# Both merge gates of a hybrid layer by a seven-product scheme, with block sums made in DRAM

## The chip, the core and the metric

The kernel runs on one core of a Trainium2 chip. The metric is the device time of one execution in microseconds (us); of several runs the median counts. One execution was also recorded by the hardware profiler, and the views of the profile quoted below are of that one.

## The reference

One layer over 512 tokens of width 1024, in float32. A gated linear recurrence (HGRN2, eight heads) and a latent attention (MLA, eight heads) run side by side on the same normed input, and two sigmoid gates of the input merge them:

```python
h   = rms_norm(x)                       # (512, 1024)
P   = h @ W_in                          # q | f | i | z_a | c_q | c_kv | k_rope | z_b | gate logits (2 * 1024)
y_a = HGRN2(q, f, i)  * silu(z_a)
y_b = MLA(c_q, c_kv, k_rope) * silu(z_b)
m   = sigmoid(g_a) * (y_a @ W_pa) + sigmoid(g_b) * (y_b @ W_pb)
out = rms_norm(x + m @ W_out)
```

## The kernel before

Every float32 operand of a large product is held as two parts, hi (rounded) and lo (the rest), and each product is three matmuls: hi by hi, hi by lo, lo by hi (`mm3`, L88). Activations are split once; `hT` is the normed input, channels on partitions, as such a pair. Weights come in pieces of 512 KB through `load_w` (L96): SP issues the transfer into one of three raw buffers (L110), ACT casts the hi part into one of four (L113), DVE subtracts to get the lo part into one of four (L114). The lines of these three steps appear in the profile for nearly every weight of the kernel.

The work goes in stages: the norm and the small compressed projection; four pairs of recurrence heads (`hg_pair`, L562: forget, value, query and gate projections, then decays, states, scores and outputs); eight attention heads (the loop at L744); the first merge gate (`gates`, L709), whose first quarter lies inside the last attention head; the product of y_a with w_pa; four steps that each do a quarter of the second gate and a quarter of y_b with w_pb (`merge`, L938); the product with w_out; the last norm.

A quarter of a gate is one `proj_ch` (L122): 256 output channels, two weight pieces, 48 matmuls that are 512 tokens wide. A gate is four of these, 192 matmuls.

The products with w_pa (`ch_product`, L870) and with w_out (`product`, L993) are already done by a seven-product scheme (Strassen's, in Winograd's form): the weight matrix and the activations are cut into 2 x 2 blocks, four sums of weight blocks and four sums of token blocks are formed, and seven products of blocks take the place of eight. For w_pa each block product is 48 matmuls of 256 tokens, seven of them 336 matmuls. The sums of weight blocks are made in SBUF: SP loads blocks into four buffers (`load_block`, L785), and POOL issues transfers that add one buffer onto another (`add_by_dma`, L800); `w_parts` (L804) then splits a sum.

What sets the order: a scheduler orders each engine's instructions by a model of time, within the limits of buffers and dependences. Places marked `manual_schedule` keep the written order, for TensorE nearly everywhere late in the kernel. `tc.issue_after(x)` keeps a transfer from being placed ahead of x. SP's queue carries the weight loads in the order in which they are issued; POOL computes small steps of its own (the scaled keys and queries of the recurrence at L472 and L484, the rope at L617 to L619, the scaling of the attention's probabilities at L683) and issues the adding transfers between them.

Of the kernel before, what the change touches and what calls it, by code (L numbers as in the profile page):

```python
# [38 lines left out]
def hybrid_layer(ctx: ExitStack, tc: tile.TileContext, a):  # L39
# [56 lines left out]
    def load_w(*pieces, lo_eng=None):  # L96

        raw = wraw.tile([P, WCH], F32, tag="raw", name="w_raw")
        hi = whi.tile([P, WCH], F32R, tag="hi", name="w_hi")
        lo = wlo.tile([P, WCH], F32R, tag="lo", name="w_lo")  # L100
# [13 lines left out]
        (lo_eng or nc.vector).tensor_tensor(lo[:, :o], raw[:, :o], hi[:, :o].bitcast(F32), op=ALU.subtract)  # L114
# [36 lines left out]
    last_split = [None]  # L151

    def split(hi, lo, src):

# [1 line left out]
        nc.vector.tensor_tensor(lo, src, hi.bitcast(F32), op=ALU.subtract)  # L156
# [319 lines left out]
    def hg_query(h, pq, pr):  # L476
# [7 lines left out]
        nc.gpsimd.tensor_tensor(c2_(q64), c4(qi)[:, :, 2:4], bc(gh, 10, 2), op=ALU.mult)  # L484
# [77 lines left out]
    def hg_pair(pair, before_gate=None, last=None):  # L562
        cc, hs = pair * 256, (2 * pair, 2 * pair + 1)
        pf = proj_ch(w_in, COL_F + cc, hT)
        kk = [hg_forget(h, pf[i]) for i, h in enumerate(hs)]
        def gate():
# [98 lines left out]
    def mla_scores(h, pool, qn, kn, qp, final=False):  # L665

        pn = []
        for i in range(NT):
# [40 lines left out]
    def gates(b, c, hook=None, to=None):  # L709

        res = []
        for i, ps in enumerate(proj_ch(w_in, COL_G + b * D + c * 256, hT, hook)):
            j = 8 * b + 2 * c + i
            g = z_tile()[:] if to is None else to[:, 2 * c + i]
            nc.scalar.activation(g, ps[:], AF.Tanh, scale=0.5, bias=hb_gate[:, j : j + 1])
            res.append(g)
        return res
# [434 lines left out]
```

## Time and profile before

| | |
|---|---|
| median of three runs | 619.11 us (618.95 to 619.19) |
| the profiled execution's own time | 619.32 us |
| its span, first to last instruction | 617.6 us |
| mean granted TensorE clock | 0.997 |
| TensorE (PE) busy | 607.3 us, 98% |
| weight loads (PEld) busy | 518.2 us, 84% |
| VectorE (DVE), ScalarE (ACT), GpSimd (POOL) busy | 400.5, 260.4, 117.9 us |
| transfers | 72.35 MB, mean 117 GB/s |

How to read the views. A group of instructions is one row: line, engine, operation, output <- inputs, shapes, count | busy time, mean ns of one | idle time of the engine just before, and what ended it. The waits of an engine are rows "engine, its output, line <- what it waited for: us in total, times, longest". The chain in order of time gives start, length and the instructions of each piece. A table by stage has for each stretch: its length, busy time of each engine with its instruction count in brackets, the TensorE clock, the share of the 16 DMA engines and GB/s. DMA queues are given with packets, MB and share of the 16 engines' time; DMA issues with KB each and the median us from issue to landing.

### The profile page before, as it was taken

The page shows a single profiled execution, that of the slowest core. Times are in us where ns is not written, and L with a number is a line of the kernel's source. Part 1 is how long each engine was busy: PE and PEld are TensorE (multiplying, and loading weights), DVE is VectorE, ACT ScalarE, POOL GpSimd, SP SyncE. Part 2 cuts the span into 40 slices and gives each one's busy share as a digit, 9 for nine tenths or more (in the row PEclk, how much of TensorE's full clock was granted, in tenths as well). Part 3 has the DMA queues.
Part 4 walks back from the last instruction along what each step waited for, and adds up shares of the span by engine and source line. Part 5 has one row for each costly group of instructions (what it writes and reads, how often), then busy time and mean ns, then how long its engine had stood idle before and what let it go on. Part 6 is the DMA issues. An engine that isn't in the chain of part 4 may idle for free.

```text
span 617.6 us, 8947 instructions
## 1 busy us (share of the span) xinstructions
PE 607.3 (98%) x3400; PEld 518.2 (84%) x3400; DVE 400.5 (65%) x633; ACT 260.4 (42%) x483; POOL 117.9 (19%) x219
## 2 busy tenths in 40 slices
PE   8999999999999999999999999999999999999995
PEld 4998888888888888888888888888899888888884
DVE  7727855498874639967677757458267742447895
ACT  5645143323144232346545555354354532334352
POOL 3106201231230032321314132101110012000021
PEclk9999999999999999999999999999999999999998
DMA  8325243223205202432232243239952799600403
GB/s 275 117 67 171 68 140 100 68 69 103 69 12 160 80 24 59 116 86 74 72 99 74 55 117 88 70 84 325 239 148 51 270 359 276 193 1 0 171 0 136
DMA packets 62377, 72.35 MB, mean 117 GB/s; under 512 B 6104, under 2 KB 48510, under 8 KB 62336
## 3 DMA queue, kind: packets, MB, share of 16 engines
q1 hardware_dynamic: 58476, 61.37, 31.9%
q0 software_dynamic: 2160, 7.87, 6.4%
q10 hardware_dynamic: 1700, 2.56, 1.4%
q8 instruction: 26, 0.43, 0.3%
q14 instruction: 15, 0.12, 0.1%
HBM read 60.25 MB, written 2.10 MB: 101 GB/s over the span
## 4 chain that ended last, share of the span: by engine, by line
PE 96%; DVE 2%; ACT 1%; DMA 0%; issue 0%; POOL 0%; POOLq 0%; ACTq 0%; DVEq 0%
PE mm_ps L90 23%; PE mm_ps L91 23%; PE mm_ps L92 23%; PE ax_ps L878 6%; PE ax_ps L986 4%; PE ax_ps L675 2%; PE mm_ps L266 2%; PE ax_ps L696 1%; PE ax_ps L536 1%; PE ax_ps L92 1%; PE ax_ps L91 1%; PE ax_ps L90 1%; PE mm_ps L878 1%; PE mm_ps L986 1%; PE ax_ps L538 1%; PE ax_ps L498 1%
## 5 line engine op out<-in xcount | busy, mean ns | idle before, releaser
L114 DVE TENSOR_TENSOR w_lo<-w_raw,w_hi 128x1024 fp32r<-128x1024 f32 (+3 forms) x86 | 101.8, 1187 | 104.9 <-ACT w_hi L113 97.7
L113 ACT CAST w_hi<-w_raw 128x1024 fp32r<-128x1024 f32 (+3 forms) x86 | 85.0, 991 | 160.0 <-PE mm_ps L91 89.7
L90 PE MATMUL mm_ps<-hT,w_hi 128*128 128x512 f32 x384 | 151.2, 394 | 0.0
L91 PE MATMUL mm_ps<-hT,w_hi 128*128 128x512 f32 x384 | 150.0, 391 | 0.0
L92 PE MATMUL mm_ps<-hT,w_lo 128*128 128x512 f32 x384 | 149.6, 391 | 0.0
L92 PEld LDWEIGHTS mm_ps<-hT,w_lo 128*128 128x128 f32 x384 | 72.1, 188 | 14.8
L90 PEld LDWEIGHTS mm_ps<-hT,w_hi 128*128 128x128 f32 x384 | 72.2, 188 | 14.5 <-DVE qn L156 0.2
L91 PEld LDWEIGHTS mm_ps<-hT,w_hi 128*128 128x128 f32 x384 | 72.2, 188 | 14.2
L92 PE MATMUL mm_ps<-w_hi,hT 128*128 128x512 f32 (+1 forms) x96 | 36.6, 383 | 0.0
L91 PE MATMUL mm_ps<-w_lo,hT 128*128 128x512 f32 (+1 forms) x96 | 36.5, 382 | 0.0
L90 PE MATMUL mm_ps<-w_hi,hT 128*128 128x512 f32 (+1 forms) x96 | 36.4, 386 | 0.0
L683 POOL TENSOR_SCALAR p<-p,sm 128x128 f32<-128x128 f32 (+3 forms) x28 | 17.0, 608 | 71.1 <-DVE sm L680 60.6
L681 ACT ACTIVATE p<-ax_ps,sm 128x128 f32<-128x128 f32 (+3 forms) x32 | 16.9, 530 | 28.0 <-DVE sm L680 26.5
L455 DVE RECIPROCAL tf<-pr 128x512 f32<-128x512 f32 x8 | 26.8, 3351 | 0.2
L90 PE MATMUL mm_ps<-yb,w_hi 128*128 128x512 f32 x64 | 24.9, 389 | 0.0
L91 PE MATMUL mm_ps<-yb,w_hi 128*128 128x512 f32 x64 | 24.9, 389 | 0.0
L92 PE MATMUL mm_ps<-yb,w_lo 128*128 128x512 f32 x64 | 24.9, 389 | 0.0
L90 PE MATMUL mm_ps<-cT,w_hi 128*128 128x512 f32 x52 | 20.7, 398 | 0.0
L92 PEld LDWEIGHTS mm_ps<-w_hi,hT 128*128 128x128 f32 x96 | 18.0, 188 | 3.0
L90 PEld LDWEIGHTS mm_ps<-w_hi,hT 128*128 128x128 f32 x96 | 18.0, 188 | 3.0
L91 PEld LDWEIGHTS mm_ps<-w_lo,hT 128*128 128x128 f32 x96 | 18.0, 188 | 2.9
L92 PE MATMUL mm_ps<-cT,w_lo 128*128 128x512 f32 x52 | 20.3, 390 | 0.0
(284 smaller groups left out, 1147.1 us busy)
## 6 DMA issues: line engine op xcount, KB each, us to landing
w_raw<-w_in SPq DMA_DIRECT2D x58, 512.0 KB, 3.8
x<-w_proj_a SPq DMA_DIRECT2D x10, 512.0 KB, 6.5
x<-x POOLq DMA_DIRECT2D x8, 512.0 KB, 9.4
w_raw<-w_proj_b SPq DMA_DIRECT2D x8, 512.0 KB, 9.9
w_raw<-w_proj_a SPq DMA_DIRECT2D x4, 512.0 KB, 11.2
ya<-w_out SPq DMA_DIRECT2D x4, 512.0 KB, 7.7
t<-w_out SPq DMA_DIRECT2D x4, 512.0 KB
yb<-w_out SPq DMA_DIRECT2D x4, 512.0 KB, 10.9
```

The lines of the kernel that those rows point to most:

```text
L90: nc.tensor.matmul(ps, lh[lsl], rh[rsl], start=start, stop=False)
L91: nc.tensor.matmul(ps, lh[lsl], rl[rsl], start=False, stop=False)
L92: nc.tensor.matmul(ps, ll[lsl], rh[rsl], start=False, stop=stop)
L113: nc.scalar.copy(hi[:, :o], raw[:, :o])
L114: (lo_eng or nc.vector).tensor_tensor(lo[:, :o], raw[:, :o], hi[:, :o].bitcast(F32), op=ALU.subtract)
L266: nc.tensor.matmul(ps, hT[l][:, 4 * kh + k, t * P : t * P + P], c_hl[kh][r][:, k * 256 : k * 256 + 256], start=kh == 0 and kind == 0 and k ...
L455: nc.vector.reciprocal(rp[:], pr[:])
L675: nc.tensor.matmul(sps[:, :n], qh[:, bl], kpe[x][:, :n], start=False, stop=x == 1)
L681: nc.scalar.activation(p[:, :n], sps[:, :n], AF.Exp, scale=SCALE, bias=sm[:, 1:2], accum_out=sm[:, 2:3])
L683: (nc.vector if final else nc.gpsimd).tensor_scalar(p[:, :n], p[:, :n], sm[:, 3:4], 0.5, op0=ALU.mult, op1=ALU.mult)
L878: nc.tensor.matmul(ps[:, o], w[k // 2][i][:, k % 2, cols], ap[j][:, k], start=not banks and c == 0 and n == 0, stop=n == 11, skip_group_ch ...
L986: nc.tensor.matmul(ps[:, o : o + n], ap[i][:, k, t * P : t * P + P], w[k // 2][j][:, k % 2, o : o + n], start=fresh and c == 0, stop=c == ...
```

## The change

Both gates are computed by the seven products. One helper, `strassen`, runs the seven block products for gate 0, gate 1 and w_pa, one after the other; w_pb then runs alone in four steps that merge, and w_out follows as before.

- **Sums of weight blocks, in DRAM.** For both gates, w_pa and w_out a `BlockSums` holds four 1 MB tiles in DRAM. `start` copies a block of the weights into each, by eight transfers of 512 KB from DRAM to DRAM on SP's queue. `add` puts an adding transfer (DRAM onto DRAM, 512 KB) on POOL's queue. Copies for gate 0 start after pair 0, for gate 1 after pair 1, for w_pa after pair 2, for w_out at attention head 1. Adds are spread over pairs 1 to 3 (gates) and heads 1 to 6. The sums are then loaded and split like any weight, through `load_w`.
- **Sums of token blocks of h, in DRAM.** `early_sums` forms them in two halves of channels, after the forget gates of pair 0 and after pair 0: twelve DVE operations and four casts each half. SP stores them (16 stores of 256 KB). After the last attention head POOL loads them back (eight loads of 512 KB).
- The sums of y's token blocks are made between gate 0 and gate 1. A gate's tanh is taken per 256 tokens. The adding transfers in SBUF, their four buffers and `w_parts` are gone; x for the residual and the output rows go into the buffers of y_a and y_b.

In the built programs 512-wide matmuls go from 1983 to 1599 and 256-wide from 520 to 1192.

```diff
+    class BlockSums:
...
+        def start(self):
+            with tc.issue_after(last_dma[0].ins):
+                for t, ij in zip(self.t, TERMS):
+                    for q in kh:
+                        nc.sync.dma_start(t[:, q], self.w[ij][:, q])
+        def add(self, *ns):
+            with tc.issue_after(last_pool[0].ins):
+                for n in ns:
+                    x = {0: self.w[0, 1], 2: self.w[1, 1], 1: self.t[0], 3: self.t[1]}[n]
+                    for q in kh:
+                        nc.gpsimd.dma_start(self.t[n][:, q], x[:, q], accum_op=ALU.add)
...
+    def early_sums(q):
...
+        e22, e21, e11, e12 = whole("qr", h22), whole("qs", h21), whole("qh", h11), whole("p3", h12)
+        minus(e22, e22, e21)
+        keep(1, "qn", e22)
+        minus_minus(e22, e22, e11)
+        keep(2, "kn", e22)
+        minus(e21, e11, e21)
+        keep(3, "qp", e21)
+        minus_minus(e12, e12, e22)
+        keep(4, "qn", e12)
+    steps = {("f", 0): lambda: early_sums(kh[0]),
+             ("f", 1): lambda: gate_w[0].add(0, 2), ("q", 1): lambda: gate_w[0].add(1), ("f", 2): lambda: gate_w[0].add(3),
+             ("q", 2): lambda: gate_w[1].add(0, 2), ("f", 3): lambda: gate_w[1].add(1), ("q", 3): lambda: gate_w[1].add(3),
+             ("h", 1): lambda: pa_w.add(0, 2), ("h", 2): lambda: pa_w.add(1), ("h", 3): lambda: pa_w.add(3),
+             ("h", 4): lambda: out_w.add(0, 2), ("h", 5): lambda: out_w.add(1), ("h", 6): lambda: out_w.add(3)}
...
+    def strassen(w, ops, out, pool, first=None, between={}):
...
+        r = ch_product(w.sum(1), s1, copied("c22", -1.0, pool))
+        ch_product(w.sum(2), s2, copied("c12", -1.0, pool), u)
+        ch_product(w.block(1, 1), s4, closed("c12", 4, 0, -1.0, out), r)
+        ch_product(w.sum(3), s3, closed("c22", 4, 1, -1.0, out), u)
+        ch_product(w.sum(4), y22, lambda b, ps: out(2 * b, 1, two(ps)), u)
...
-                first_gates = gates(0, 0, lambda: pts.extend(hook()))
+                u = ch_product(w11, h11, copied("c11", 1.0))
+                ch_product(w21, h12, lambda b, ps: later.append((b, ps)), tile=mm_tile, hook=lambda: pts.extend(hook()))
                 mla_out(h, pts, v, z)
...
+    for n, s in ((1, s1), (2, s2), (4, s4), (3, s3)):
+        for i in range(2):
+            nc.gpsimd.dma_start(s[i][:], h_dram[n - 1][i][:])
...
+        strassen(gate_w[0], h_ops, gate_out(0, lambda j: ma[:, j]), gp, first=u)
...
+        strassen(gate_w[1], h_ops, gate_out(1, lambda j: g1[j]), gp,
...
+        strassen(pa_w, (q1, q2, q3, s1, s2, s3, s4), gated, gp)
...
-        for i, (g, ps) in enumerate(merge(1, c, ybs, a["w_proj_b"][0])):
+        for i, ps in enumerate(proj_ch(a["w_proj_b"][0], c * 256, ybs)):
```

The order on three engines changes where the steps were put in. On SP, around the end of pair 0: before, the loads of the weights of pair 0's last projections and of pair 1's first ones follow one another (w_raw is a raw buffer).

```order
L110 DMA w_raw<-w_in 128x4x256 [waits DMAHW2_49,DVE_49]
L110 DMA w_raw<-w_in 128x4x256 [waits DMAHW3_49,DVE_49]
L110 DMA w_raw<-w_in 128x4x256 [waits DMAHW4_49,DVE_49]
L110 DMA w_raw<-w_in 128x4x256 [waits DMAHW5_49,DVE_49]
L110 DMA w_raw<-w_in 128x4x256 [waits DMAHW6_49,DVE_49]
```

In the changed program (g_t is a DRAM tile of gate 0's sums, h a DRAM tile of token sums, qn and kn what is stored) the same place reads:

```order
L110 DMA w_raw<-w_in 128x4x256 [waits DMAHW3_49,DVE_49]
L738 DMA g_t_647<-w_in 128x2x512 [waits DMAHW4_49]
L775 DMA h_666<-kn_808 128x512 [waits DMAHW5_49,DVE_49]
L738 DMA g_t_647<-w_in 128x2x512 [waits DMAHW6_49]
L738 DMA g_t_648<-w_in 128x2x512 [waits DMAHW7_49]
L738 DMA g_t_648<-w_in 128x2x512 [waits DMAHW0_49]
L738 DMA g_t_649<-w_in 128x2x512 [waits DMAHW1_49]
L738 DMA g_t_649<-w_in 128x2x512 [waits DMAHW2_49]
L775 DMA h_670<-qn_822 128x512 [waits DMAHW3_49,DVE_49]
L738 DMA g_t_650<-w_in 128x2x512 [waits DMAHW4_49]
L738 DMA g_t_650<-w_in 128x2x512 [waits DMAHW5_49]
L110 DMA w_raw<-w_in 128x4x256 [waits DMAHW6_49]
```

The last row is pair 1's first weight piece: all eight copies of gate 0 and two stores have moved in between it and the last load of pair 0.

On DVE, in pair 0, behind the forget gates of its second head: before, the key scalings are followed by the lo parts of the query weights and by the query steps (L481 to L485).

```order
L455 RECIPROCAL tf<-pr 128x512 [waits DVE_49]
L470 TENSOR_TENSOR ki<-k,tf 128x512 [waits DVE_49]
L471 TENSOR_TENSOR ko<-ki,pr 128x512 [waits DVE_49]
L473 TENSOR_TENSOR k_759<-ko,gh_641 128x512 [waits DVE_49,Pool_49]
L114 TENSOR_TENSOR w_lo<-w_raw,w_hi 128x1024 [waits DMAHW2_49,Activation_49]
L114 TENSOR_TENSOR w_lo<-w_raw,w_hi 128x1024 [waits DMAHW3_49,Activation_49]
```

In the changed program the sums (L720, L724, L768) and their lo parts (L156) stand between the same steps:

```order
L455 RECIPROCAL tf<-pr 128x512 [waits DVE_49]
L724 SCALAR_TENSOR_TENSOR qr<-qr,qh 128x512 [waits DVE_49]
L156 TENSOR_TENSOR qp_815<-qs,qp_814 128x512 [waits Activation_49]
L470 TENSOR_TENSOR ki<-k,tf 128x512 [waits DVE_49]
L724 SCALAR_TENSOR_TENSOR p_797<-p_797,qr 128x512 [waits DVE_49]
L768 TENSOR_TENSOR qh<-hT_125,hT_126 128x512
L114 TENSOR_TENSOR w_lo<-w_raw,w_hi 128x1024 [waits DMAHW2_49,Activation_49]
L768 TENSOR_TENSOR qs<-hT_125,hT_126 128x512 [waits DVE_49]
L156 TENSOR_TENSOR kn_808<-qr,kn_807 128x512 [waits Activation_49]
L471 TENSOR_TENSOR ko<-ki,pr 128x512 [waits DVE_49]
```

The two lo parts of the query weights now come behind eight to ten further rows. Some twenty rows on, ahead of the second head's query step (L483), stands the lo part of the second half's first sum, which waits for a store to be done (DMAHW3 is the semaphore of the store of h_670 above):

```order
L502 SCALAR_TENSOR_TENSOR st<-st,ft,ax_ps 128x128 [waits DVE_49]
L156 TENSOR_TENSOR qn_1253<-qr,qn_1252 128x512 [waits DMAHW3_49]
L483 TENSOR_TENSOR qi<-f,pr 128x512 [waits DVE_49]
```

So the query's scaling, qi, is queued behind that store.

On POOL, in pair 3 and ahead of the first head's rope: before, the scaled keys and queries and the rope follow one another.

```order
L472 TENSOR_TENSOR k_2212<-ko,gh_641 128x256 [waits DVE_49,PE_49]
L484 TENSOR_TENSOR q_2352<-qi,gh_637 128x256 [waits DVE_49]
L484 TENSOR_TENSOR q_2361<-qi,gh_641 128x256 [waits DVE_49]
L617 TENSOR_TENSOR qr<-qr,qtab 128x512 [waits DMAHW3_49,DMAHW5_49,DMAHW2_49,DMAHW7_49,DMASW0_49,Activation_49]
L618 TENSOR_TENSOR qs<-qs,qtab 128x512
```

In the changed program (line numbers of the rope are two higher) four adding transfers of gate 1 stand between them, each waiting for transfers that it reads or adds onto (DMASW are those of POOL's queue):

```order
L472 TENSOR_TENSOR k_2346<-ko,gh_643 128x256 [waits DVE_49,PE_49]
L745 DMA g_t_652<-g_t_651 128x1024 [waits DMAHW6_49,DMASW1_49]
L745 DMA g_t_652<-g_t_651 128x1024 [waits DMAHW7_49,DMASW2_49]
L484 TENSOR_TENSOR q_2488<-qi,gh_639 128x256 [waits DVE_49]
L484 TENSOR_TENSOR q_2497<-qi,gh_643 128x256 [waits DVE_49]
L745 DMA g_t_654<-g_t_652 128x1024 [waits DMAHW2_49,DMASW7_49,DMASW5_49]
L745 DMA g_t_654<-g_t_652 128x1024 [waits DMAHW3_49,DMASW6_49,DMASW0_49]
L619 TENSOR_TENSOR qr<-qr,qtab 128x512 [waits DMAHW5_49,DMAHW3_49,DMAHW7_49,DMAHW2_49,Activation_49]
```

Queries and rope now stand behind the waits of those four.

More of the change, by code (lines that the diff above doesn't have):

```diff
@@ L94, in hybrid_layer, with load_w @@
     last_dma = [None]
[L96 removed]
+    def load_w(*pieces, to=None):
         raw = wraw.tile([P, WCH], F32, tag="raw", name="w_raw")
[L99 to L100 removed]
+        hi, lo = to or [pool.tile([P, WCH], F32R, tag=tag, name=f"w_{tag}")[:] for pool, tag in ((whi, "hi"), (wlo, "lo"))]
         views, o = [], 0
@@ L706, in mla_out @@
         nc.vector.tensor_tensor(yb[:, h], ops[:], z[:], op=ALU.mult)
[L709 to L717, printed above, removed]
+    kh = [slice(0, 2), slice(2, 4)]
+    half_t = [slice(0, 256), slice(256, 512)]
@@ L719, in hybrid_layer, with step, beside @@
+    def step(*at):
+        if at in steps:
+            steps[at]()
+    def beside(pair):
+        if pair < 2:
+            gate_w[pair].start()
+        if pair == 0:
+            early_sums(kh[1])
+        if pair == 2:
+            pa_w.start()
     for pair in range(H // 2 - 1):
         hg_pair(pair)
+        beside(pair)
     early = []
@@ new lines, in hybrid_layer, with copied, done, closed @@
+    two = lambda ps: ps[:].rearrange("p (c t) -> p c t", c=2)
+    part = {}
+    def copied(key, sign, pool=None):
+        def done(b, ps):
+            if b == 0:
+                t = pool.tile([P, WCH], F32, "part", 2) if pool else wraw.tile([P, WCH], F32, tag="raw", name=key)
+                part[key] = t[:].rearrange("p (b c t) -> p b c t", b=2, c=2)
+            nc.scalar.activation(part[key][:, b], two(ps), AF.Copy, scale=sign)
+        return done
+    def closed(key, j, tok, sign, out):
+        def done(b, ps):
+            t = part[key][:, b]
+            nc.vector.scalar_tensor_tensor(t, two(ps), sign, t, op0=ALU.mult, op1=ALU.add)
+            out(j + 2 * b, tok, t)
+        return done
@@ L739, in hybrid_layer @@
+    h11, h12, h21, h22 = zip(*[blocks(t) for t in hT])
     mw = Pool("mla", "right")
@@ new lines, in hybrid_layer, with gate_out, out @@
+    q1, q2, q3 = [[yo.tile([P, 4, 256], F32R, f"q{n}{i}") for i in range(2)] for n in range(1, 4)]
+    mp = Pool("merged", "left")
+    ma = mp.tile([P, KD, S], F32, "ma")
+    gp = Pool("gates", "left")
+    g_rows = gp.tile([P, 5, S], F32, "g_rows")
+    def gate_out(b, rows):
+        def out(j, tok, src):
+            for i in range(2):
+                n = 8 * b + j + i
+                nc.scalar.activation(rows(j + i)[:, half_t[tok]], src[:, i], AF.Tanh, scale=0.5, bias=hb_gate[:, n : n + 1])
+        return out
@@ new lines, in hybrid_layer @@
+    g1 = {j: z_tile()[:] for j in (0, 1, 4)}
+    for n, j in enumerate((2, 3, 5, 6, 7)):
+        g1[j] = g_rows[:, n]
+    with tc.manual_schedule(engines={mybir.EngineType.PE}):
+        strassen(gate_w[1], h_ops, gate_out(1, lambda j: g1[j]), gp,
+                 between={3: lambda: a_parts(y22, s1), 4: lambda: a_parts(y11, s2), 5: lambda: a_parts(y12, s4),
+                          6: lambda: a_parts(y21, s3)})
+    ybs = hT
+    for h in range(H):
+        split(ybs[0][:, h], ybs[1][:, h], yb[:, h])
```

273 lines of the change are left out of this document (113 added, 160 removed).

## The prediction

> **What bounds the kernel now.** I read the summary first, then the chain of work that ended last by engine.
>
> ```profile
> span 617.6 us, 8947 instructions
> PE 607.3 (98%) x3400; PEld 518.2 (84%) x3400; DVE 400.5 (65%) x633; ACT 260.4 (42%) x483; POOL 117.9 (19%) x219
> ...
> PE 96%; DVE 2%; ACT 1%; DMA 0%; issue 0%; POOL 0%; POOLq 0%; ACTq 0%; DVEq 0%
> ```
>
> TensorE is busy for 98% of the span and carries 96% of the chain. Next, the waits of TensorE, all of them:
>
> ```profile
> PE ax_ps L231 <- DVE zero L277: 1.2, 1, 1.2
> PE ax_ps L255 <- DVE xn L247: 0.8, 2, 0.4
> PE mm_ps L266 <- DVE w_lo L238: 0.5, 1, 0.5
> PE mm_ps L266 <- ACT hT L257: 0.2, 1, 0.2
> ```
>
> Together 2.7 us, every one at lines of the opening (norm, transposes, first projection). From there to the last product TensorE never waits. So a change pays exactly the matmul time it removes, less whatever waits it brings into a stream that has none. Last, the chain in order of time, through the one matrix product that is already done by seven products at 256 tokens (L878), and the first products of the output projection (L986), whose matmuls are 512 wide:
>
> ```profile
> 444.45 5.75 PE ax_ps L878 x48
> 450.20 5.76 PE mm_ps L878 x48
> 455.96 25.92 PE ax_ps L878 x216
> ...
> 482.58 2.87 PE ax_ps L878 x24
> ...
> 571.84 5.44 PE ax_ps L986 x24
> 577.28 5.44 PE mm_ps L986 x24
> 582.72 21.77 PE ax_ps L986 x96
> ```
>
> The seven products are 48 + 48 + 216 + 24 = 336 matmuls in 5.75 + 5.76 + 25.92 + 2.87 = 40.30 us, 119.9 ns each. A 512-wide matmul takes 5.44 / 24 = 226.7 ns. Half the width costs 53% of the time, not 50%.
>
> **The gain.** A gate now is four pieces of 48 matmuls, 192 x 226.7 ns = 43.52 us. By seven products it is 336 x 119.9 ns = 40.30 us. That is 3.22 us a gate, 6.44 us for both. The seven products of w_pa and of w_out are there before and after. All else must stay hidden, and the next paragraphs go through it.
>
> A rule of the Trainium skill ("TensorE: Matmul & The Clock Gate", section "Back-to-back issue gap") gives N / 2.4 + 2.5 ns for the isolated gap, estimated at 215.8 and 109.2 ns here, which would make the gain 9.5 us. The rows above show more for both widths, and relatively more for the narrow one. The same section warns that the sustained gap is set by weight load and matmul together; the next rows agree.
>
> ```profile
> core 0: us, PE busy (x) PEld busy (x) DVE busy (x) ACT busy (x) POOL busy (x), PEclk, DMA share, GB/s
> 66.50:108.70 42.20, 42.20 (x264) 35.16 (x262) 27.01 (x34) 14.30 (x19) 6.47 (x15) 1.00 0.35 100
> 85.00:400.00 315.00, 314.97 (x1862) 268.04 (x1861) 211.91 (x362) 126.63 (x275) 75.75 (x136) 1.00 0.29 81
> 444.40:485.45 41.05, 41.05 (x341) 40.92 (x340) 26.35 (x37) 19.64 (x25) 1.74 (x2) 1.00 0.45 115
> 485.45:571.84 86.39, 86.39 (x382) 71.54 (x382) 46.29 (x55) 33.68 (x45) 5.32 (x6) 1.00 0.60 183
> ```
>
> In 444 to 485 us weight loading is busy 40.92 of 41.05 us: narrow matmuls run at the pace of their weight loads. The clock is 1.00 there as elsewhere, so I expect 119.9 ns to hold for the gates too.
>
> **The gate products themselves.** Each set of seven products brings 14 weight pieces of 512 KB (14 casts, 14 subtracts), the work that closes four quadrants, and 16 tanh halves. The same row (444 to 485) has w_pa's set with DVE at 26.35 and ACT at 19.64 of 41.05 us. The gates exchange DVE's gating for ACT's tanh:
>
> ```profile
> L715 ACT ACTIVATE z<-mm_ps,hb_gate 128x512 f32<-128x512 f32 x10 | 6.9, 685 | 5.8 <-PE mm_ps L92 5.6
> ```
>
> 16 halves at no more than a whole one's 0.685 us are at most 11 us more of ACT, 31 of 41; DVE stays at or below 26. Weights are fetched at 1 MB per 5.75 us, 182 GB/s, and the row for 485 to 572 us has 183 GB/s now without a wait of TensorE. No cost. Its cover is the lookahead of three raw and four split pieces; without it a late piece would cost up to one landing, some 4 us. The rearranged tail of the last head (24 narrow matmuls of 2.88 us in place of 12 wide ones of 2.72 between the transposes and the head's output) covers the same splits: nothing. What goes is 14 adding transfers into SBUF that ran beside w_pa and w_out; they had no wait of TensorE to their name, so nothing is gained either.
>
> **Token sums, 24 DVE and 8 ACT operations.** They stand in pair 0, half behind the forget gates and half behind the pair.
>
> ```profile
> L156 DVE TENSOR_TENSOR kn<-mm_ps,kn 128x512 fp32r<-128x512 f32 x8 | 5.5, 682 | 0.0
> ...
> 84.21 1.23 DVE L114 TENSOR_TENSOR w_lo<-w_raw,w_hi 128x1024 fp32r<-128x1024 f32 x1 [2.29 <-ACT w_hi L113]
> ...
> 105.86 1.15 PE L512 MATMUL ax_ps<-qi,ki 128*64 128x64 f32 x32
> 106.94 0.70 PE L518 MATMUL ax_ps<-qi,ko 128*32 128x32 f32 x32
> 107.57 1.15 PE L523 MATMUL ax_ps<-q,k 128*64 128x64 f32 x16
> 108.64 0.50 PE L90 MATMUL mm_ps<-hT,w_hi 128*128 128x512 f32 x1
> ```
>
> 24 x 0.682 = 16.4 us. Between 66.5 and 108.7 us DVE is busy 27.0 of 42.2 us, so it would have 43.4 us of work: 1.2 us too much. TensorE would feel it at pair 0's scores (105.86), which need qi, or at pair 1's first product (108.64), which needs the low part of its weights. One sum of the second half also waits for a store of the first half, in the queue behind copies, and qi is queued behind it on DVE. I take a wait of 1.3 us. Bounds: 0, if only part of the sums comes before the scores, and 2.5, if the wait for that store adds as much again.
>
> **Copies from DRAM to DRAM, 32 of 512 KB on SP's queue.** No row of this kernel shows such a transfer. Nearest are these:
>
> ```profile
> q1 hardware_dynamic: 58476, 61.37, 31.9%
> q0 software_dynamic: 2160, 7.87, 6.4%
> ...
> w_raw<-w_in SPq DMA_DIRECT2D x58, 512.0 KB, 3.8
> ...
> x<-x POOLq DMA_DIRECT2D x8, 512.0 KB, 9.4
> ```
>
> SP's queue moved 61.37 MB in 31.9% of 617.6 us, 197 us of all engines: 311 GB/s, 1.7 us for 512 KB. A load alone lands 3.8 us after its issue. These are my two ends. The first eight copies stand ahead of pair 1's first weights. They go out when a raw buffer comes free, at the end of the subtract at 84.21 us, so at 85.4. At 1.7 us each those weights land at 85.4 + 13.4 + 3.8 = 102.6; they must be there by 108.64 less a cast and a subtract, 2.3 us, so 106.3. No wait. At 3.8 us each, one after the other, it is 119.6 and a wait of 13 us. I take 1.7, because eight in flight are a queue's rate and not a lone landing. The other three groups are issued with up to six pieces (three raw, three split) of 5.44 us each, 33 us of products, ahead of their need; there even 3.8 us each (30.4 us) just hides.
>
> **Adds in DRAM, 32 of 512 KB on POOL's queue.** POOL's queue moved 7.87 MB in 6.4%, 39.5 us: 199 GB/s, 2.6 us for 512 KB. Its median landing is 9.4 us after issue. In DRAM both the read and the write are far, so I take 2.6 to 5.3 us (twice), with 9.4 as the outer end. Traffic of 85 to 400 us then is 0.29 x 315 = 91 us, plus 32 x 1.7 = 54, plus 32 x 2.6 to 5.3 = 84 to 168: 73 to 99% of the 16 engines' time: tight at the upper end, not over.
>
> ```profile
> L802 POOL DMA_DIRECT2D x<-x x8 | 7.1, 966 | 63.6 <-PE mm_ps L91 33.8 <-DMA x<-w_proj_a 21.4 <-DMA x<-x 8.3
> ...
> L675 PE MATMUL ax_ps<-kpe,qp x64: 220/334/398, 273.7 to 401.9; 128*128 128x128 f32 x16, 128*128 128x256 f32 x16, 128*128 128x384 f32 x16, 128*128 128x512 f32 x16
> ...
> 254.36 0.62 POOL L484 TENSOR_TENSOR q<-qi,gh 128x256 f32<-128x256 f32 x1 [2.09 <-DVE qi L483]
> 260.12 1.27 POOL L617 TENSOR_TENSOR qr<-qr,qtab 128x512 f32<-128x512 f32 x1 [5.13 <-DMA qs<-qr]
> ```
>
> POOL spends 0.97 us to issue one; 40 (with eight loads of token sums) are 39 us, against 75.75 of 315 us busy. But each add waits on POOL for the add or copy it reads. Behind it stand the scaling of the probabilities, pair keys and queries, and the rope. Between pair 3's last query (254.98) and the rope (260.12) POOL idles 5.13 us, room for two issues. The scores of eight heads start from 273.7 to 401.9 us: 128.2 / 7 = 18.3 us a head at most. Eight adds are spread over three heads, 55 us, so POOL is held only if one takes over 6.9 us. At 2.6 to 5.3 it isn't: no cost. The token sums come back after the last scores, at 402 us, and are needed at the third product; the two before it take 5.75 us each, so at least 11.5 us against 9.4: no cost.
>
> **The sum.** 619.32 (the profiled run: span 617.6 and 1.7 around it) - 6.44 + 1.3 = 614.2. The median of the three runs, 619.11, lies 0.2 lower: 614.0.
>
> **The rivals.**
>
> *Slower: adds that hold POOL.* If an add in DRAM takes more than 6.9 us of sustained time, POOL runs behind through heads 1 to 6. The next head's scaled probabilities come late, then its transposes, and TensorE waits in each head. At 8 us it is 8 x (8 - 6.9) = 9 us for each of two matrices, 18 together: 612.7 + 18 = 631; at the landing row's 9.4, 8 x 2.5 x 2 = 40: 653. Point from which it decides: 6.9 us an add. For it: 9.4 us stands in the trace, and POOL is in order, so one late add blocks much. Against it: that figure is a latency with other adds in flight, and the rate of the same queue is 2.6. Chance 0.14.
>
> *Slow copies at pair 1.* At 3 us a copy pair 1's weights land at 85.4 + 24 + 3.8 = 113.2, 7 us late: 612.7 + 7 = 619.7, no change to speak of. It decides from 2.15 us a copy (17.1 us for eight). For it: read and write share the same memory. Against it: the loads' rate leaves 20% of room, and the queue is all but empty then. Chance 0.13.
>
> *DVE becomes the bound in pair 0.* If sums overlap badly with the scans and casts, the 1.2 us of overload becomes 4 us, because each sum goes through a split that waits for ACT: 617. For it: 43.4 us of work in 42.2. Chance 0.09.
>
> *Narrow matmuls at half price.* Were the gates' narrow matmuls 113.3 ns (half of 226.7), 672 of them take 76.2 us, and the gain is 10.9: 619.1 - 10.9 = 608.2, or 609.5 with the wait. The rule of the Trainium skill above would lie near this. Against it: 119.9 over 336 of them in this trace. Chance 0.03.
>
> That the change doesn't do what it says is out: in the built programs 512-wide matmuls go from 1983 to 1599 and 256-wide from 520 to 1192, which is 2 x 192 less and 2 x 336 more.
>
> **How the numbers follow.** The forecast has 0.61, own range 612.3 (no new wait, 612.7, less 0.4 of scatter) to 616.5 (waits of 2.5 us in pair 0, and one late piece of up to 1.3). For the range I add DVE's case (617) and most of the slow copies, up to 3.1 us each: 620.5. Left out are the slow adds (0.14), the half price (0.03) and the rest of the copies (0.03), 0.20 together. A measurement of this kernel can tell about 0.2%, 1.2 us, from no change: faster is below 617.9, slower above 620.35. Faster: 0.61 + 0.07 of DVE's case + 0.03 of the copies + 0.03 = 0.74. Same: 0.02 + 0.07 + 0.01 = 0.10. Slower: 0.13 of the adds + 0.03 of the copies = 0.16.
>
> **What would show it.** Right: both gates' seven products at 40.3 us each with nothing between; TensorE's waits longer by one to three lines around 104 to 112 us; POOL's waits on adds not named by any TensorE wait. Wrong: a wait of TensorE at pair 1's first product of over 3 us that leads to SP's weight load (copies); waits on the scaled probabilities or the rope in heads 1 to 6 (adds); gate matmuls off 119.9 ns, or a clock below 1.00 in them.

## The result, and the profile after

The changed kernel takes 655.57 us (median of six runs, 651.63 to 661.24); the kernel before took 619.08. One of the six runs of the kernel before, 757.71 us, was a slow one and is outside the ratio. The ratio is 1.0593, with a 95% interval of 1.0541 to 1.0645. The forecast, 614.0 in a range of 612.3 to 620.5, said faster and not slower, and missed by 41.6 us.

The head of the page of the profile after, with the shares of the chain:

```profile
span 653.2 us, 9792 instructions
...
PE 614.3 (94%) x3688; PEld 534.9 (82%) x3688; DVE 431.2 (66%) x679; ACT 285.0 (44%) x531; POOL 143.8 (22%) x245
...
PE 43%; DMA 9%; DVE 5%; ACT 3%; issue 2%; POOL 2%; ACTq 0%; POOLq 0%; SPq 0%; DVEq 0%
```

TensorE's share of the chain falls from 96% to 43%, and transfers enter it with 9%. (The shares listed here add up to 64%, those before to 99%, so they rank the engines and no more.) The span grew by 653.2 - 617.6 = 35.6 us. TensorE is idle for 653.2 - 614.3 = 38.9 us instead of 10.3, which is 28.6 more. It is busy for 7.0 us more although it has 6.4 us less to do, so 13.4 us went to slower matmuls. -6.4 + 28.6 + 13.4 = 35.6. (In e5 below, which has the same matmuls and makes no sums, TensorE is busy for 601.1 us, 13.2 less than here.)

The longest waits of TensorE (before, nothing stood here but the opening's 2.7 us):

```profile
PE mm_ps L91 <- DVE z L558: 11.4, 1, 11.4
PE ax_ps L701 <- POOL p L685: 5.4, 2, 3.8
PE ax_ps L536 <- DVE asb L527: 4.9, 2, 4.7
PE ax_ps L840 <- ACT w_hi L113: 2.1, 2, 1.6
```

The longest, at the first attention head, can be followed in the timeline (start, length, what; in brackets the idle time before and what ended it):

```profile
268.58 12.03 SPq L738 DMA_DIRECT2D out_t<-w_out  x8
274.67 1.27 POOL L619 TENSOR_TENSOR qr<-qr,qtab 128x512 f32<-128x512 f32 x1 [5.43 <-DMA qs<-qr]
280.70 4.82 ACTq L625 DMA_DIRECT2D qs<-qr  x2
285.56 1.24 ACT L630 CAST qp<-qr 64x512 fp32r<-64x512 f32 x2 [15.20 <-DMA qs<-qr]
286.83 1.04 ACT L113 CAST w_hi<-w_raw 128x1024 fp32r<-128x1024 f32 x1
...
294.42 0.79 PE L91 MATMUL mm_ps<-w_hi,cT 128*128 128x512 f32 x1 [11.39 <-DVE z L558]
```

SP needs 12 us to issue w_out's eight copies, 6.2 of them in waits for earlier loads to land. The rope's first small transfers were issued from 264 us on; POOL, which waits for them, starts at 274.67 and has done its three steps by 278.5. ACT issues the rope's second transfers only at 280.70 and needs 4.8 us for two. ACT does its work in order, so it stands for 15.2 us, with a cast of weights behind the rope's cast, and TensorE waits in the end. Which engine the wait is put down to (DVE) is only the last link.

The chain in order of time names what held ACT's issue:

```profile
261.69 8.93 DMA w_raw<-w_in
270.63 10.01 DMA out_t<-w_out
280.70 4.85 DMA qs<-qr
```

A copy of w_out lands at 280.64 and releases the rope's transfer, though the code gives the two no data in common. The lists under "The change" show how that can be: each transfer waits for one of the numbers DMAHW0 to DMAHW7, which SP's transfers take in turn, and POOL waits for the rope's transfers by such numbers too. So a transfer can have to wait until the one that had its number before has landed, whatever that one carries. The same link stands ahead of other late ropes: a load of attention weights ahead of the third rope here (landed at 349.8 us) and in f1 below (346.0), a copy of w_out ahead of the fourth in m5 (371.9). Releasers are inferred from semaphores, and no run gave the rope numbers of its own, so this link is read and not tested.

The rope's transfers also land later once they are issued. Those of the whole kernel, from issue to landing (least, median, most; 2.1, 2.5 and 3.9 us in the kernel before):

```profile
DMA to landing us min/median/max: 2.4/6.6/9.5
```

The clock behind such a gap, and the load of the DMA engines ahead of it, in stretches of the changed kernel (last three columns: granted clock, share of the 16 DMA engines, GB/s):

```profile
210.00:220.00 10.00, 9.94 (x113) 8.00 (x112) 4.13 (x9) 1.55 (x2) 0.00 (x0) 1.00 1.10 225
220.00:225.00 5.00, 1.56 (x7) 0.94 (x5) 1.82 (x3) 2.58 (x3) 0.00 (x0) 0.91 0.54 172
225.00:230.00 5.00, 3.77 (x18) 3.80 (x19) 2.23 (x4) 0.35 (x2) 0.00 (x0) 0.50 0.17 39
265.00:275.00 10.00, 10.00 (x119) 8.66 (x118) 6.18 (x14) 1.96 (x4) 1.96 (x3) 1.00 1.10 254
...
295.00:300.00 5.00, 5.00 (x19) 4.48 (x18) 2.13 (x8) 0.46 (x2) 0.00 (x0) 0.58 0.16 35
```

Ahead of each gap the DMA engines are full (1.10 as the profile counts it); behind it TensorE runs at half clock for about 5 us. Up to the first attention scores the changed kernel is 23.4 us late (297.1 us against 273.7), 16.1 us of it the waits of 11.4 and 4.7 us, and most of the rest the clock. Another 5.5 us are lost from there to the last scores and 6.7 behind them, where the 6.4 us should have been gained.

### The profile page after: what moved, and what is told of

It is laid out like the page before. It is cut to its first block, busy times and chain, and to the rows that moved or that the text cites. A ratio compares the mean times of both kernels' runs of the same rounds, so it can differ in the third digit from the quotient of the medians.

```text
span 653.2 us, 9792 instructions
## 1 busy us (share of the span) xinstructions
PE 614.3 (94%) x3688; PEld 534.9 (82%) x3688; DVE 431.2 (66%) x679; ACT 285.0 (44%) x531; POOL 143.8 (22%) x245
## 3 DMA queue, kind: packets, MB, share of 16 engines
q0 software_dynamic: 7952, 21.50, 17.4%
## 4 chain that ended last, share of the span: by engine, by line
PE 43%; DMA 9%; DVE 5%; ACT 3%; issue 2%; POOL 2%; ACTq 0%; POOLq 0%; SPq 0%; DVEq 0%
PE ax_ps L840 15%; PE mm_ps L91 7%; PE mm_ps L92 7%; PE mm_ps L93 6%; DMA qs<-qr 3%; DMA w_raw<-w_ukv 3%; PE mm_ps L840 3%; DMA out_t<-w_out 2%; DVE w_lo L114 1%; DMA w_raw<-w_in 1%; PE ax_ps L677 1%; PE ax_ps L701 1%; DVE ya L1057 1%; ACT w_hi L113 1%; PE ax_ps L91 1%
## 5 line engine op out<-in xcount | busy, mean ns | idle before, releaser
L114 DVE TENSOR_TENSOR w_lo<-w_raw,w_hi 128x1024 fp32r<-128x1024 f32 (+3 forms) x116 | 135.2, 1180 | 106.9 <-ACT w_hi L113 101.4
L113 ACT CAST w_hi<-w_raw 128x1024 fp32r<-128x1024 f32 (+3 forms) x116 | 114.7, 1005 | 133.0 <-DMA w_raw<-w_in 37.5
L91 PE MATMUL mm_ps<-hT,w_hi 128*128 128x512 f32 x320 | 126.3, 396 | 0.5 <-ACT tf L449 0.5
L92 PE MATMUL mm_ps<-hT,w_hi 128*128 128x512 f32 x320 | 125.4, 392 | 0.0
L93 PE MATMUL mm_ps<-hT,w_lo 128*128 128x512 f32 x320 | 124.9, 392 | 0.0
L91 PEld LDWEIGHTS mm_ps<-hT,w_hi 128*128 128x128 f32 x320 | 60.3, 189 | 13.3 <-ACT tf L449 0.9
L92 PEld LDWEIGHTS mm_ps<-hT,w_hi 128*128 128x128 f32 x320 | 60.3, 188 | 11.7
L840 PE MATMUL ax_ps<-s,w_hi 128*128 128x256 f32 x384 | 55.8, 289 | 2.1 <-ACT w_hi L113 2.1
L840 PEld LDWEIGHTS ax_ps<-s,w_hi 128*128 128x128 f32 x384 | 51.2, 197 | 2.5 <-ACT w_hi L113 2.5
L92 PE MATMUL mm_ps<-w_lo,hT 128*128 128x512 f32 (+1 forms) x96 | 36.5, 382 | 0.0
L840 PE MATMUL ax_ps<-s,w_lo 128*128 128x256 f32 x192 | 32.5, 291 | 1.1 <-DVE w_lo L114 1.1
L840 PEld LDWEIGHTS ax_ps<-s,w_lo 128*128 128x128 f32 x192 | 27.6, 199 | 1.6 <-DVE w_lo L114 1.6
L156 DVE TENSOR_TENSOR pt<-ax_ps,pt 128x512 fp32r<-128x512 f32 (+1 forms) x24 | 13.7, 591 | 14.1 <-ACT pt L155 14.1
L93 PEld LDWEIGHTS mm_ps<-w_hi,hT 128*128 128x128 f32 x96 | 18.0, 188 | 3.0
## 6 DMA issues: line engine op xcount, KB each, us to landing
out_t<-w_out SPq DMA_DIRECT2D x8, 512.0 KB, 13.4
```

The source lines that it names most:

```text
L91: nc.tensor.matmul(ps, lh[lsl], rh[rsl], start=start, stop=False)
L92: nc.tensor.matmul(ps, lh[lsl], rl[rsl], start=False, stop=False)
L93: nc.tensor.matmul(ps, ll[lsl], rh[rsl], start=False, stop=stop)
L113: nc.scalar.copy(hi[:, :o], raw[:, :o])
L114: nc.vector.tensor_tensor(lo[:, :o], raw[:, :o], hi[:, :o].bitcast(F32), op=ALU.subtract)
L840: nc.tensor.matmul(ps[:, o], w[k // 2][i][:, k % 2, cols], ap[j][:, k], start=not banks and c == 0 and n == 0, stop=n == 11, skip_group_ch ...
```

## Experiments

The theory after the result: the transfers that make the sums come in bunches that fill the DMA engines, and what has little lead (weights, the rope's small transfers) lands late; the clock then adds to the longer waits. The rivals: adds hold POOL (the prediction's own slower case); the token sums load DVE in pair 0; the gates' products themselves are slower than counted; or the amount of traffic counts, wherever it is put. All kernels are edits of the changed one. Times are medians of four to eleven runs, those of before 618.98 to 619.2 beside them. The code cuts show the lines that matter; "..." marks what is left out.

**e1: no sums made.**

```diff
-                        nc.sync.dma_start(t[:, q], self.w[ij][:, q])
...
-                        nc.gpsimd.dma_start(self.t[n][:, q], x[:, q], accum_op=ALU.add)
...
-            return self.load(self.t[n - 1], to)
+            return self.load(self.w[TERMS[n - 1]], to)
...
-    steps = {("f", 0): lambda: early_sums(kh[0]),
...
-            nc.gpsimd.dma_start(s[i][:], h_dram[n - 1][i][:])
```

> The changed kernel without anything that makes sums: no copies, no adds, no token sums (the places of the sums are taken by plain blocks of the weights and of h, so that all products, loads and splits stay; the output is not the reference's). If the loss comes from making the sums, this is 619.1 - 6.4 = 612.7 us, 612 to 614, with no wait of TensorE behind the opening. If narrow matmuls or the closing work of the gates are slower than w_pa's, it stays above 616.

Measured: 618.8 us, ratio 0.9988 (0.9979 to 0.9997). Ten runs fall in two groups, four at 617.3 us and six at 618.9; most of the 6.4 us is gone in both, before any sum is made. The number is that of the rival, but not for its reason: the waits do it, not slow matmuls (169 narrow ones in 20 us below, as counted). Its waits, and its stretches around the longest one and in gate 1:

```profile
PE ax_ps L91 <- DVE pt L156: 1.6, 1, 1.6
...
PE ax_ps L1017 <- DVE ya L1051: 0.9, 1, 0.9
PE ax_ps L834 <- DVE w_lo L114: 0.8, 1, 0.8
...
PE ax_ps L834 <- ACT w_hi L113: 0.5, 1, 0.5
```

```profile
394.00:396.00 2.00, 0.76 (x4) 0.79 (x5) 2.00 (x7) 0.46 (x2) 0.00 (x0) 1.00 0.59 154
396.00:398.00 2.00, 2.00 (x8) 1.71 (x7) 1.98 (x10) 0.89 (x3) 0.00 (x0) 0.54 0.29 113
398.00:400.00 2.00, 2.00 (x8) 1.62 (x8) 0.26 (x1) 0.34 (x2) 0.00 (x0) 0.61 0.00 0
...
460.00:480.00 20.00, 20.00 (x169) 20.00 (x168) 11.09 (x13) 11.98 (x18) 0.00 (x0) 1.00 0.62 180
```

A wait of 1.6 us for the last splits of the probabilities is followed by 4 us at 0.54 and 0.61 of the clock, a loss of some 1.7 us. This trace is of a run of 618.77 us. e8 below has the same wait in a trace of 617.57 us, and there the clock stays at 1.00; so the two groups seem to be runs with and without this loss (mean granted clock 0.995 in each of the six, 0.996 to 0.998 in the four). In the kernel before, 27 matmuls of the first gate stood at this place, between the splits and their use; in e1 the order has none there. The first block product uses the ax banks of PSUM, which the last head's scores and transposes hold; the plain gate used the mm banks.

**e5: the bank pools exchanged,** on e1.

```diff
-                u = ch_product(w11, h11, copied("c11", 1.0))
-                ch_product(w21, h12, lambda b, ps: later.append((b, ps)), tile=mm_tile, hook=lambda: pts.extend(hook()))
+                u = ch_product(w11, h11, copied("c11", 1.0), tile=mm_tile)
+                ch_product(w21, h12, lambda b, ps: later.append((b, ps)), hook=lambda: pts.extend(hook()))
```

> e1 (no sums made) with one edit: gate 0's first block product goes to the three mm banks of PSUM and the second to the ax banks, instead of the other way round. Theory: in e1 the first product cannot start before the scores of the last head have left the ax banks, so 27 gate matmuls that stood between head 6's splits and their use in the kernel before are gone from there, and TensorE waits 1.6 us and runs at half clock behind it. Then the wait on pt (L156) goes and the time is 3 us below e1: 615.5. If the wait comes from DVE having more to do, it stays and the time equals e1.

Measured: 614.72 us, ratio 0.9929 (0.9911 to 0.9946). 4.1 us below e1's median, 2.6 below its faster group: the wait of 1.6 us on pt is gone with the lower clock behind it, one of 0.8 us in gate 0 too, and 34 narrow matmuls stand where the 27 wide ones did. 4.4 of the counted 6.4 us are there; 1.4 of the rest are two waits that its trace still shows, in gate 0 and at the last product.

**e6: the sums of y later,** on e5 (moved from between the gates to behind gate 1's third product).

> e5 with the token sums of y moved from between the gates to behind gate 1's third product. Theory: DVE is busy without a break from 420 to 442 us in e1, and the lo parts of gate 0's weights queue behind the sums of y; moved, TensorE's 1.3 us of waits in gate 0 go: 614.2. Rival: the work only moves and the same waits appear in gate 1: equal to e5.

Measured: 614.65 us, ratio 0.9928 (0.9912 to 0.9943): equal to e5. e5's only wait left in gate 0 was one of 0.5 us, not 1.3, so there was little to find. The rival has the number, but not its reason: the 0.5 us stay in gate 0 (at 435 us) and no wait appears in gate 1.

**e2: token sums alone,** on e1 (their steps, stores and loads put back).

> As e1 plus the token sums with their stores and loads; no copies, no adds (weight blocks in place of weight sums). DVE-bound pair 0 (the prediction's term): 1.3 us over e1, at most 2.5. Traffic theory: under 1 us over e1, because the changed kernel shows TensorE waits of only 0.7 us up to 200 us.

Measured: 622.75 us, ratio 1.0057 (1.0042 to 1.0072), 3.95 over e1, more than either theory said. The waits:

```profile
PE ax_ps L837 <- ACT w_hi L113: 2.1, 2, 1.6
...
PE ax_ps L837 <- DVE w_lo L114: 1.4, 2, 1.2
```

They lie at 420 to 425 us, in gate 0, behind the loads that bring the sums back; pair 0 shows none. From 424 to 432 us TensorE then runs at 0.50 to 0.66 of the clock. The stretch of those loads, with the DMA engines 0.87 busy:

```profile
400.00:420.00 20.00, 19.76 (x162) 19.42 (x160) 10.09 (x17) 10.02 (x20) 3.15 (x6) 1.00 0.87 289
```

**e8: token sums not brought back,** on e2 (the loads left out).

> e2 without bringing the token sums back (sums of h made and stored in pair 0, plain blocks of h used in the gates; no copies, no adds). Theory: the 3.95 us that e2 costs over e1 are the 4 MB of loads that meet gate 0's first weights, not the DVE work in pair 0, so this is e1's 618.8, within 0.7. The prediction's DVE term says 1.3 us over it or more: 620 to 623.

Measured: 617.82 us, ratio 0.9984 (0.9974 to 0.9994): 4.9 below e2 and 1.0 below e1. Its ten runs fall in groups like e1's, most at 617.7 and three at 619.4, each 0.4 us above the one of e1; the 1.0 comes of more runs in the faster group. So making and storing the sums costs about 0.4 us and not 1.3; bringing 4 MB back as gate 0 starts costs 4 to 5 us. Of these, 2.2 are longer waits in gate 0 (3.5 us in e2, 1.3 here), and the clock behind them is worth about 3, an estimate from the stretches of e2. What makes the weights late is only half shown. Here the same stretch has 0.40:

```profile
400.00:420.00 20.00, 20.00 (x166) 19.87 (x165) 12.10 (x18) 11.76 (x22) 0.00 (x0) 1.00 0.40 122
```

In e2 ACT's order has six casts of y ahead of two casts of weights that e8 does first. Whether those weights would have landed in time is open.

**e3: copies alone,** on e2.

> As e2 plus the 32 copies, loaded back as the sums; no adds. If adds that hold POOL are the cause, this equals e2. If the traffic and SP's queue are the cause (copies ahead of weights and of the rope's small transfers), the wait at attention head 1 stays, 5 to 11 us with as much as 5 us of lower clock behind it, and the time is 618 to 632.

Measured: 626.91 us, ratio 1.0124 (1.0092 to 1.0156): 4.2 over e2, with runs from 624.2 to 629.3. The trace is of the longest; at the first head it has the wait that the changed kernel has:

```profile
PE mm_ps L91 <- DVE z L558: 5.6, 1, 5.6
```

**e4: adds alone,** on e2.

```diff
-                        nc.gpsimd.dma_start(self.t[n][:, q], x[:, q], accum_op=ALU.add)
+                        nc.gpsimd.dma_start(h_all[n][:, q], x[:, q], accum_op=ALU.add)
```

> As e2 plus the 32 adds, put onto the stored token sums in DRAM in place of the copies' tiles; no copies (the token sums are thereby changed, and weight blocks stand for weight sums). If adds that hold POOL are the cause, the time is that of the changed kernel, 645 to 656. If it takes copies and adds together, this is 614 to 630, and the two parts e3 - e2 and e4 - e2 add up to less than the 42 us that the changed kernel lies above e2.

Measured: 627.26 us, ratio 1.0136 (1.0119 to 1.0153): 4.5 over e2. Copies and adds apart cost 4.2 + 4.5 = 8.7; together 655.57 - 622.75 = 32.8. Neither hurts much by itself. That slow adds alone hold POOL falls: all adds are in e4, and it is 28 us faster than the changed kernel. What e4 doesn't have is adds that wait for copies. Those are in the changed kernel, and POOL's waits for them are given below.

**m1: the changed kernel with its transfers spread.** Copies two at a time, adds two at a time, part of w_out's adds and half of the token sums later.

```diff
-             ("f", 1): lambda: gate_w[0].add(0, 2), ("q", 1): lambda: gate_w[0].add(1), ("f", 2): lambda: gate_w[0].add(3),
...
+             ("f", 1): lambda: (g0.add(0), g0.copy(1)), ("q", 1): lambda: (g0.add(2), g0.copy(3)),
+             ("f", 2): lambda: (g0.add(3), g1w.copy(1)), ("q", 2): lambda: (g1w.add(0), g1w.copy(3)),
...
```

> The changed kernel, whole and with all its sums, with only the transfers' places changed: copies two at a time (one tile per step) instead of eight, adds two at a time instead of four, none right ahead of the first rope, three of w_out's four add steps in gate 1 and w_pa, half of the token sums brought back behind gate 0's third product. If bunched transfers make the loss (copies cost 4.2 us and adds 4.5 us apart, 32.8 together, over e2), this falls from 655 to 622 to 632. If the amount of traffic makes it, it stays over 645.

Measured: 634.21 us, ratio 1.0243 (1.0226 to 1.0259), 21.4 less with the same bytes (114.4 MB), and 2.2 above the range that was expected.

**m2: m1 with the edits of e5 and e6.**

> m1 with the edits of e5 and e6. 4.6 us below m1 if those waits are the same ones here: 617 to 628. Below 617.9 it would beat the kernel before.

Measured: 631.28 us, ratio 1.0200 (1.0184 to 1.0216), 2.9 below m1, and above the range that was expected. Up to the first attention scores it now loses nothing (273.6 us against 273.7 before), with the DMA engines three to four fifths busy:

```profile
104.00:160.00 56.00, 56.00 (x397) 47.24 (x397) 43.87 (x52) 19.42 (x39) 22.57 (x47) 1.00 0.80 223
160.00:210.00 50.00, 50.00 (x268) 42.16 (x262) 32.12 (x39) 15.81 (x33) 15.11 (x27) 1.00 0.83 205
```

The rope's transfers land late there too (2.2 / 5.2 / 7.6 us), so a late landing alone is not yet a loss. Against e5 it loses 8.8 us up to the last scores and 9.0 from there to the end.

**f1: only w_out's copies spread,** in the changed kernel.

```diff
-            if h == 1:
-                out_w.start()
+            if h in (1, 2, 3, 4):
+                out_w.copy((0, 2, 1, 3)[h - 1])
```

> The changed kernel with one edit: w_out's eight copies go out two at a time in attention heads 1 to 4 instead of all at head 1. Theory: they delay the first rope's small transfers, ACT waits for those in order with weight casts behind it, and TensorE waits 11.4 us and then runs at about half clock; with them gone from there, 17 us less: 635 to 641. If traffic in total is what counts, or the adds of gate 1 that run at the same time, it stays above 648.

Measured: 647.39 us, ratio 1.0448 (1.0420 to 1.0477): 8.2 us less, not 17. The wait of 11.4 us is gone, but TensorE's waits for the probabilities from POOL have grown from 5.4 us (behind the third and fourth rope) to 8.7 (behind the third):

```profile
PE ax_ps L701 <- POOL p L685: 8.7, 3, 5.4
```

At the first scores f1 is 12.2 us ahead of the changed kernel, at the last scores 6.0: part of the loss has moved on to a later rope.

**m3: half of the change.** Gate 0 by plain products, the rest as m2 without e5's and e6's edits, transfers mostly ahead of the heads.

> Half of the change: gate 0 by plain products as before, gate 1, w_pa and w_out with sums in DRAM; copies and adds two at a time, all but w_out's ones during the recurrence, where m2 showed no TensorE wait; token sums brought back during gate 0's plain products. The gain is 3.2 us of TensorE; the gate's filler in the last head is as before; left are w_out's copies and adds in the heads and the tail's 0.9 us. Theory of bunched traffic: 616.5 to 619.5, not slower than before. If the amount of traffic matters (three quarters of it is left), it is 625 or more.

Measured: 624.84 us, ratio 1.0080 (1.0065 to 1.0095). That is 5 us above the range, and just what the rival of sheer traffic said; m4 below tells the two apart. No wait of TensorE in the recurrence, but the last scores come at 408.5 us (401.9 before). One add was issued some 5 us ahead of the first rope's transfers, another some 4 us ahead of the third's. The rope's transfers land after 2.1 / 2.5 / 3.9 us (least, median, most) in the kernel before and after 2.2 / 3.8 / 6.5 in m3.

**e9 and e10: one add, ahead of a rope and behind it,** on e5 (the line is e9's; e10 has head 3 in it). Both also make the copy of 1 MB that the add goes onto, behind pair 0.

```diff
+    steps = {("h", 2): lambda: gate_w[0].add(0)}
```

> e5 (no sums; 614.7) plus one copy of 1 MB behind pair 0 and one add of 1 MB at attention head 2, some 5 us ahead of the third rope's transfers; the sum is not used. Rope theory: the rope's 64 KB transfers land 2 to 3 us later, POOL holds the probabilities back, TensorE waits 1 to 2 us and may lose as much again by the clock: 616.5 to 618.5. If only the sum of bytes counts, 614.7 to 615.2.

> The same add at attention head 3, behind the third rope. Rope theory: 614.7, no new wait. If the traffic counts wherever it is, equal to e9.

Measured: e9 618.63 us, ratio 0.9994 (0.9985 to 1.0003); e10 615.50, ratio 0.9942 (0.9928 to 0.9955). The same 1 MB costs 3.9 us over e5 ahead of the rope and 0.8 behind it. Rope theory had said 616.5 to 618.5 and 614.7. e9's eleven runs go from 617.7 to 619.8, and the trace is of the longest. The rope's start on POOL, in e9 and in e10 (0.43 us of waiting in e5):

```profile
327.98 1.30 POOL L619 TENSOR_TENSOR qr<-qr,qtab 128x512 f32<-128x512 f32 x1 [3.42 <-DMA qs<-qr]
```

```profile
324.52 1.29 POOL L619 TENSOR_TENSOR qr<-qr,qtab 128x512 f32<-128x512 f32 x1 [0.39 <-DMA qs<-qr]
```

e9's rope transfers, the waits of TensorE that follow, and the clock:

```profile
DMA to landing us min/median/max: 2.0/3.2/6.2
```

```profile
PE ax_ps L701 <- POOL p L685: 2.0, 2, 1.4
```

```profile
335.00:340.00 5.00, 5.00 (x23) 4.56 (x23) 3.63 (x6) 4.06 (x9) 0.00 (x0) 0.70 0.39 98
```

In e10 the slowest lands after 4.2 us, and there is no such wait. ACT issues the third rope's transfers at 319.8 us in e9 and 319.4 in e10, so the issue isn't late here; the transfers are slower, with a median of 6.1 us from issue to landing around this rope, against 3.1 in e10 and 2.2 in e5. So a 64 KB transfer on ACT's queue lands later when an add is in flight; POOL waits for it with the probabilities' scaling behind; TensorE waits 2.0 us and loses some more at 0.70 of the clock.

**m4: m3 with its adds away from the ropes.**

```diff
-             ("h", 2): lambda: (pa_w.add(3), out_w.copy(1)), ("h", 4): lambda: (out_w.add(0), out_w.copy(3))}
...
+             ("h", 1): lambda: pa_w.add(3), ("h", 2): lambda: out_w.copy(1), ("h", 3): lambda: out_w.add(0),
+             ("h", 4): lambda: (out_w.add(2), out_w.copy(3))}
```

> m3 with its adds kept away from the ropes (none issued within 10 us ahead of one). Rope theory: 5 of the 6.6 us that m3 loses in the heads go: 618.5 to 620.5. Otherwise 623 to 625 as m3.

Measured: 618.87 us, ratio 0.9996 (0.9987 to 1.0005), 6.0 below m3 with the same bytes (102.8 MB). The last scores are at 402.2 us again, and the rope's transfers are as they were:

```profile
DMA to landing us min/median/max: 2.0/2.4/3.7
```

Of half the gain, 3.2 us, next to nothing shows: its trace has 0.7 and 0.8 us of new waits, in gate 0 and at the last product; where the rest goes is open.

**m5: m2 with its adds away from the ropes.**

> m2 (631.3; both gates, all sums) with its adds kept away from the ropes in the same way. Rope theory: most of the 8.8 us that m2 loses in the heads go: 622 to 626. The 8.5 us that it loses in the gates stay.

Measured: 634.2 us, ratio 1.0247 (1.0230 to 1.0264), 2.9 above m2: the expectation failed. Kept from the ropes, the adds bunch up in the room that is left:

```profile
PE mm_ps L91 <- DVE z L558: 5.5, 2, 4.7
```

The 4.7 us lie at 374 us, behind six adds and six copies issued between 330 and 355 us, and POOL waits 10.3 us for the fourth rope's transfers there. The copies had not been moved out of the ropes' way, so m5 does not show that the whole traffic cannot be placed; it shows that this placing is no better. No placing tried here made the whole change faster than the kernel before: the best, m2, is 12.1 us above it and 16.6 above e5. How much of that is places and how much sheer traffic is open.

## Why the prediction was wrong, point by point

- **TensorE bounds the kernel and never waits.** Right, and used the wrong way round: with no wait to remove, every new wait is paid in full, and the longer ones by the clock a second time.
- **The gain, 3.2 us a gate.** Right as a price. In e1's gate 1, 169 narrow matmuls take 20 us, 118 ns each, against the 119.9 that were taken.
- **"The rearranged tail of the last head ... covers the same splits: nothing."** Wrong, 4.1 us (e1 against e5; 2.6 without the clock's part). The comparison was of lengths, 2.88 against 2.72 us; it looked at the place behind the last transposes and not at the 27 matmuls one head earlier that the new banks kept away.
- **Token sums, 1.3 us in pair 0.** Wrong place. DVE made them in pair 0 without a wait of TensorE there, for some 0.4 us in all (e8); the loads that bring them back, which the prediction put at no cost because 9.4 us is less than 11.5, cost 4 to 5 us (e2 against e8). Their need was checked, but not what else was due at that time.
- **Copies.** At pair 1, where the prediction feared them, they cost next to nothing: from 62 to 160 us TensorE is idle for 0.5 us. "The other three groups ... up to six pieces of 5.44 us" failed: attention's pieces are of 64 to 256 KB and last a shorter time, so the lead is less, and w_out's group met the first rope. Alone, 4.2 us (e3).
- **Adds.** The rate was within its bounds: POOL's queue moved 21.50 MB in 17.4% of 653.2 us, 189 GB/s or 2.8 us for 512 KB. The loads of the token sums are in that; e2's queue, which has them and no adds, moved 4.72 MB in 2.2% of 621.0 us, which leaves 3.1 us for an add.

```profile
q1 hardware_dynamic: 65100, 89.69, 43.6%
q0 software_dynamic: 7952, 21.50, 17.4%
```

  POOL's own waits ahead of adds are these rows, 10.7 us, and no wait of TensorE names an add.

```profile
POOL g_t L745 <- DMA g_t<-w_in: 5.1, 2, 3.6
POOL g_t L745 <- issue: 2.3, 1, 2.3
POOL g_t L745 <- DMA g_t<-g_t: 1.7, 1, 1.7
POOL pa_t L745 <- DMA pa_t<-w_proj_a: 1.6, 1, 1.6
```

  The prediction's slower rival gave 631 to 653 us and so came near the result, but by a mechanism that the runs do not show: ahead of TensorE's waits for the probabilities POOL stood for the rope's transfers, not for an add:

```profile
356.69 1.29 POOL L619 TENSOR_TENSOR qr<-qr,qtab 128x512 f32<-128x512 f32 x1 [11.64 <-DMA qs<-qr]
```

  The prediction showed this wait in the kernel before, 5.13 us ahead of the first rope, and read it as room for two issues; it is a wait for transfers, which more traffic lengthens.
- **"73 to 99% ... tight at the upper end, not over."** This is the step that failed: traffic that fits on the average was put at no cost. The average was fair (0.73 from 85 to 400 us); the engines take it in bunches, with stretches of 1.05 to 1.10 and others of 0.05. Bytes were the same in m1, and 21.4 us less were paid. The price of a transfer was taken as its own bytes; what it costs is the delay of whatever short transfer is due beside it (e9 against e10: 3.1 us for the same add), by a slower landing and, where eight copies stand in a row, by a later issue. That the 3.9 us of e9 would grow to 36.5 for the whole change is not added up from parts; m1's 21.4 us are the part that bunches are shown to have.
- **The clock** was expected at 1.00. 13.4 of the 35.6 us are matmuls at a lower one, behind the waits.

## What to carry to other kernels

Where TensorE never waits, a background transfer has no price by itself: ask for each small transfer and each weight with short lead what will be in flight when it is issued, and keep adds and copies out of the time just ahead of it (m4 kept its adds 10 us away), because one late transfer on an in-order engine's path stalls everything behind. Look in the order lists, too, for what a small transfer's issue waits for: it can be a large copy that shares nothing with it but a semaphore. Check which PSUM banks a product uses when it is put in another's place: its matmuls may have been the filler of somebody else's wait. And before trusting a counted gain, build the version without its side costs first (here e1 and e5): it shows in one run what the gain is worth at best.

## What the runs showed of the hardware

- The clock behind a short gap of TensorE is not settled by the gap's length. A wait of 1.61 us was followed by 4 us at 0.54 and 0.61 in e1, and by 1.00 at the same place in e8 and e2. Two of 0.6 and 1.4 us within 2.4 us gave 0.70 in the next 5 us (e9). Waits of 0.8, 0.9 and 1.1 us, 2 to 3 us apart, left it at 1.00 (f1, 284 to 291 us). The changed kernel's 11.4 and 4.7 us were each followed by some 5 us at 0.50 to 0.58. The Trainium skill ("TensorE: Matmul & The Clock Gate", section "Why this matters for your kernels") warns of idle gaps over some 3 us; the two long ones agree, and in e1 and e9 a lower clock followed shorter ones too.
- A transfer of 64 KB on ACT's queue lands up to 6.2 us after issue with a 1 MB add in flight on POOL's, against 3.8 without (e9, e5; around the same rope 6.2 against 2.5). The Trainium skill ("DMA: Bandwidth & Descriptors", section "Queues, rings and completion order") says that an engine takes turns between queues by packets; taking turns did not keep the small one on time.
- SP's eight copies of w_out took 12.0 us to issue (w_proj_a's eight, at 185 us, 7.6), and ACT's own issue, whose data were ready when POOL's rope ended at 278.5 us, came at 280.70, as one of them landed. By the chain and the order lists this is a wait of the program, for a semaphore that both use; no run tests it.
- Copies and adds cost 4.2 and 4.5 us apart and 32.8 together; why they multiply so is followed in the trace for the rope and the weights at the first head, and not for every microsecond of it. The rope's transfers land after 2.5 us in the median in e2, 3.7 with copies, 3.3 with adds, 6.6 with both.
